# A convolution-and-attention trunk: two issues moved to another queue, four weight splits moved to another engine, one cost raised in the planner

## The chip, the cores and the metric

The kernel runs on one core of one Trainium2 chip. The metric is the device time of one execution in microseconds (us). Engines are named as in the profile: PE (TensorE), PEld (its weight loads), DVE (VectorE), ACT (ScalarE), POOL (GpSimd) and SP (SyncE, which only issues transfers). An engine's name with a q (ACTq, SPq) stands for its sequencer.

## The reference

One sequence of 512 tokens, width 1024, two layers, all in float32. Cut to its calls:

```python
for layer in range(2):
    if layer == 1:
        k_nope, k_rope, v = mla_shared_kv(h, ...)
    hn = rms_norm(h, mix_pre_g[layer])
    if layer < 1:
        m = conformer_conv(hn, ...)      # h @ w_pw1, gate, 31 taps per channel, layer norm, silu, @ w_pw2
    else:
        m = mla_attention(hn, ...)       # 8 heads, block-causal mask, softmax
    h = h + rms_norm(m, mix_post_g[layer])
    f = jnp.square(jax.nn.relu(rms_norm(h, ffn_pre_g[layer]) @ w_ff1[layer])) @ w_ff2[layer]
    h = h + rms_norm(f, ffn_post_g[layer])
```

In `conformer_conv` the product with `w_pw1` (1024 by 2048) gives a value half and a gate half; value times sigmoid(gate) goes through a causal convolution of 31 taps along the tokens, each channel by itself.

## The kernel before

**Split numbers.** Each float32 operand of a large matmul is held as a high part (`wh`, a rounded copy that ACT makes) and a lower part (`wl`, the rest). A product is three matmuls: high by high, lower by high, high by lower. Weights come in blocks of 128 by 1024 (512 KB) into five `raw` tiles; there are five `wh` tiles and six `wl` tiles. The function `weight` makes the lower part in one of two ways:

- DVE subtracts: `split` records an ACT copy of each 512 columns (raw to wh) and a DVE `tensor_tensor` (raw minus wh to wl).
- By transfer: ACT writes the rounded negative into `wl` and the rounded positive into `wh`, and then POOL issues a transfer that adds the block from DRAM onto `wl`.

The first pointwise weights are 16 blocks named `pw1`; block index 2c is the value half of channel group c (128 channels), and 2c+1 is its gate half. `lo_by_dma(name)` is true for all of `pw1`. Blocks 0 to 3 go the first way and blocks 4 to 15 the second.

**The convolution.** Eight channel groups c = 0 to 7. Groups 0, 1 and 3 take their 31 taps on DVE (`taps_vector`). Groups 2, 4, 5, 6 and 7 (`T_BLOCKS`) take them on PE (`taps_tensor`, 72 matmuls a group): the group's tokens must first be dealt so that four token phases lie side by side on the partitions. `deal_tokens` does this through DRAM: one 256 KB transfer writes the group's `u` to a `dealt` buffer, and when that has landed four 64 KB transfers read it back into `uu`. ACT issues both steps. An engine's instructions run in program order, so ACT stands still while one of these issues waits. The taps also need a matrix of weights: `load_toeplitz` loads nine 256 KB tiles for a group (`big<-cw` in the trace) on SP. `TAPS_AFTER` says where in PE's order the taps stand: group 2 after the products of c = 4, group 4 after c = 6, groups 5 and 6 after c = 7, and group 7 at the end, before the layer norm.

**Who orders the work.** The kernel does not issue instructions directly. A `Program` records them, `Program.cost` gives each an estimated duration in ns, and `schedule` simulates the five engines with those estimates and a simple model of transfers; of 16 rounds it keeps the order with the shortest simulated span, and `run` issues that order. Hence a changed estimate, or another engine for an operation, can change the order on every engine anywhere in the kernel. In the model a transfer is not placed more than `LEAD` = 16 us before it is due; on the chip SP issues as soon as its waits are met. All instructions carry the line of the one call that issues them (L640), so the trace is read by tiles and not by lines.

**Attention.** For each of 8 heads and 4 query blocks DVE adds the mask to the scores and reduces them to a row maximum in one `tensor_tensor_reduce`, and a DVE `tensor_scalar` on one column multiplies that maximum by a per-row weight.

Of the kernel before, what the change touches and what calls it, by code (L numbers as in the profile page):

```python
# [87 lines left out]
def lo_by_dma(name):  # L88
    if name[0] == "ff1":
        return name[2] == 0 and name[3] < 4  # L90
    if name[0] == "ff2":
        return name[1] == 0 and name[2] == 3 and name[3] in LAST_BY_DMA
    return name[0] in ("pw1", "pw2")
# [168 lines left out]
def _size(ap):  # L262
    n = 1
    for _, c in list(ap.ap)[1:]:
        n *= c
    return n
# [17 lines left out]
class Program:  # L284
# [68 lines left out]
    def cost(self, engine, method, kwargs, outs, ins):  # L353
        n = max([_size(a) for a in outs + ins] or [1])
        if method == "dma_start":
            return {"scalar": 380.0, "gpsimd": 900.0}.get(engine, 400.0)
        apart = {"vector": 0.77, "scalar": 0.6}.get(engine, 0.0) * n if any(
            list(a.ap)[-1][0] > 1 for a in outs + ins if _size(a) > 8
        ) else 0.0
        if engine in ("scalar", "vector") and ins and _size(ins[0]) > 8 and ins[0].ap[0][1] < P:  # L360
            apart += 120.0 if engine == "scalar" else 97.0
        if engine == "tensor":
            n = _size(outs[0])
            if ins[0].dtype == F32R:
                k = ins[0].ap[0][1]
                return max(120.0, n / 2.4 + 13.7) + (200.0 if k < P else 0.0)
            return 109.0 if method == "transpose" else max(222.0, n / 0.6 + 9)
        few = sum(_size(a) == 1 for a in ins) if n > 8 else 0
        psum = any(a.tensor.space == PSUM for a in outs + ins)
        if engine == "vector":  # L370
            wide = [a for a in ins if _size(a) > 1]
            rate = 1.042 if len(wide) > 1 or psum else 0.521
            return 68 + rate * n + 62 * few + apart
        if engine == "scalar" and n == 1:

            return 1350.0
        if engine == "scalar":
            few += "accum_out" in kwargs
            return (51 if psum else 94) + 0.833 * n + 93 * few + apart
        if engine == "gpsimd":  # L380
            return 150 + 2.1 * n
        return 450.0
# [68 lines left out]
    def schedule(self, tags):  # L451
# [49 lines left out]
        def better(op, e, cost, now):  # L501

            for f, _, _, _, c, held in op.ways:
                if f != e:
                    queue = sum(o.cost for _, _, o in avail[f] if not o.done and o is not op and o.rank < op.rank)
                    done = max(clock[f], now, port[0] if held else 0.0) + queue + c
                    if done < now + cost or (c > cost and done + SLACK < op.rank):
                        return True
            return False

        def urgent(op, e, cost, now):

            if op.held > HOLD or op.cost < 200:
                return False
            return any(
                at < now + 145 and not o.done and o.cost < TINY and o.rank < op.rank for at, _, o in future[e]
            )
# [126 lines left out]
def trunk(ctx: ExitStack, tc: tile.TileContext, xT, xN, wts, vec, along, rope, cw, out):  # L644
# [3 lines left out]
    nc = Program(tc.nc)  # L648
# [32 lines left out]
    n = VEC["mix_pre0"] + KT  # L681
# [35 lines left out]
    def scaled(name, src):  # L717

        lo, hi = ([big(F32R) for _ in range(2)] for _ in range(2))
        for o in range(2):  # L720
            raw = big()
            nc.sync.dma_start(out=raw, in_=src[:, o * T : (o + 1) * T])
            g0 = VEC[GAINS[name[0]]] + 4 * o
            gain = vt[:, g0 : g0 + 4].rearrange("p (k o) -> p k o", o=1).to_broadcast([P, 4, P])
            nc.vector.tensor_tensor(
                out=raw.rearrange("p (k m) -> p k m", m=P), in0=raw.rearrange("p (k m) -> p k m", m=P), in1=gain, op=ALU.mult
            )
            split(raw, slice(0, T), (hi[o], lo[o]))
        return hi, lo

    def weight(key):

        while key not in blocks:
            name, parts = USE[len(blocks)]
            i, n = BLK[parts[0][0]], _cols[BLK[parts[0][0]]]
            if name[0] in GAINS:
                blocks[name] = scaled(name, wts[i])
                continue
            raw, hi, lo = nc.tile(RAW), nc.tile(WH, F32R), nc.tile(WL, F32R)
            step = 256 if i < 2 else n  # L740
            for o in range(0, n, step):
                nc.sync.dma_start(out=raw[:, o : o + step], in_=wts[i, :, o : o + step])
            for other, sign in parts[1:]:
                if sign > 0:
                    nc.gpsimd.dma_start(out=raw, in_=wts[BLK[other]], accum_op=ALU.add)
                else:
                    second = nc.tile(RAW)
                    nc.sync.dma_start(out=second, in_=wts[BLK[other]])
                    for o in range(0, n, 512):
                        nc.vector.tensor_tensor(  # L750
                            out=raw[:, o : o + 512], in0=raw[:, o : o + 512], in1=second[:, o : o + 512], op=ALU.subtract
                        )
            src = raw if len(parts) > 1 else wts[i]
            if i >= 4 and lo_by_dma(name):

                for o in range(0, n, 512):
                    for dst, scale in ((lo, -1.0), (hi, 1.0)):
                        nc.scalar.activation(dst[:, o : o + 512], raw[:, o : o + 512], AF.Copy, scale=scale)
                nc.gpsimd.dma_start(out=lo, in_=src, accum_op=ALU.add)
            else:  # L760
                step = 256 if i < 2 else min(n, 512)
                engines = VG if name[0] in ATT else ("vector",)
                for o in range(0, n, step):
                    split(raw, slice(o, o + step), (hi, lo), engines=engines)
            blocks[name] = hi, lo
        return blocks[key]
# [5 lines left out]
    def products_of(keys, X, t0, n, nk=KT):  # L772

        w = [weight(key) for key in keys]
        pts = [nc.tile(MM) for _ in keys]
        for k in range(nk):
            for (hi, lo), pt in zip(w, pts):
                ks = slice(k * P, (k + 1) * P)
                if isinstance(hi, list):
                    hi, lo, ks = hi[k // 4], lo[k // 4], slice(k % 4 * P, (k % 4 + 1) * P)  # L780

                for j, (a, b) in enumerate(((hi, X[k][0]), (lo, X[k][0]), (hi, X[k][1]))):
                    nc.tensor.matmul(
                        pt[:, :n], lhsT=a[:, ks], rhs=b[:, t0 : t0 + n],
                        start=(k == 0 and j == 0), stop=(k == nk - 1 and j == 2),
                    )
        return pts

    def split(src, s, dst, d=None, engines=("vector",)):

        d = s if d is None else d
        nc.scalar.activation(dst[0][:, d], src[:, s], AF.Copy)
        nc.binary(engines, out=dst[1][:, d], in0=src[:, s], in1=dst[0][:, d].bitcast(F32), op=ALU.subtract)
# [167 lines left out]
    def feed_forward(layer, X, F):  # L961
# [6 lines left out]
        for q in range(4):  # L968
# [29 lines left out]
            def sides(q, p):  # L998
                return [weight(("ff2", layer, q, p, u)) for u in range(2)]
# [151 lines left out]
    def deal_tokens(c, up):  # L1151
        uu = UU[T_BLOCKS.index(c) % 3]
        dr = nc.tile(DEALT)
        nc.scalar.dma_start(out=dr.rearrange("p r m -> p (r m)"), in_=up)
        for r in range(R):
            nc.scalar.dma_start(
                out=uu[32 * r : 32 * r + 32, :, 8:], in_=dr[:, r, :].rearrange("(g c) m -> c g m", g=GROUPS)
            )

# [33 lines left out]
    for c in range(KT):  # L1193
# [5 lines left out]
        for j in T_BLOCKS:  # L1199
            if TAPS_AFTER.get(j) == c:  # L1200
                n = T_BLOCKS.index(j)
# [17 lines left out]
        if CONV[c] == "V":  # L1219
            taps_vector(c, u)  # L1220
        else:
            deal_tokens(c, u)
# [473 lines left out]
```

## Time and profile before

| | |
|---|---|
| median of three runs | 1064.88 us (1062.82 to 1067.0) |
| the profiled execution's own time | 1068.46 us |
| its span, first to last instruction | 1066.7 us |
| PE busy | 1045.5 us, 98% of the span |
| DVE, ACT, POOL busy | 764.1, 640.9, 141.6 us |
| mean granted PE clock | 0.993 of full speed |
| queue q1 (SP's), 16 engines' share | 40.9%, 150.15 MB |
| queue q0 (POOL's) | 25.6%, 49.29 MB |
| queue q10 (ACT's) | 1.1%, 3.68 MB |

The span is 1.8 us shorter than the profiled execution's own time, and that execution is 3.6 us above the median. A busy PE is not a PE at its peak: at a lower granted clock the same matmuls take longer and PE still counts as busy.

### The profile page before, as it was taken

The numbers are of one execution on the slowest core, as the hardware profiler recorded it, in microseconds if no ns is written. First come the engines' busy times: TensorE is split into PE (matmuls) and PEld (weight loads), VectorE is DVE, ScalarE is ACT, GpSimd is POOL, SyncE is SP. The second block draws the span as 40 slices with busy tenths as digits, with TensorE's granted clock in tenths as the row PEclk, the third lists the DMA queues.
The fourth block names the chain that finished last, engine by engine and source line by source line (L and its number), as shares of the span: only waits on it lengthen the run. The fifth ranks groups of instructions, "written<-read, shape, count | busy, mean of one in ns | idle before, by whom it ended". The sixth has DMA issues, their size and how long they took to land. (4 is left out here: it accounts for less than half of the span.)

```text
span 1066.7 us, 15181 instructions
## 1 busy us (share of the span) xinstructions
PE 1045.5 (98%) x5284; PEld 884.7 (83%) x5284; DVE 764.1 (72%) x1559; ACT 640.9 (60%) x1343; POOL 141.6 (13%) x165
## 2 busy tenths in 40 slices
PE   8989999999999999999999999999999999999996
PEld 7878988988888888888888888889888888888885
DVE  6497994857438737959988987547574495497698
ACT  8543497766545446545767877558565554454652
POOL 1110011100100100001104533301010010000010
PEclk9989999999999999999999999999999999999998
DMA  9995888657866848658923132557599388485684
GB/s 288 300 254 171 287 211 236 156 168 207 253 171 190 257 126 241 189 182 227 237 69 93 56 100 81 174 182 179 161 245 253 112 235 257 143 243 168 187 237 129
DMA packets 67613, 204.08 MB, mean 191 GB/s; under 512 B 7632, under 2 KB 13904, under 8 KB 67536
## 3 DMA queue, kind: packets, MB, share of 16 engines
q1 hardware_dynamic: 49680, 150.15, 40.9%
q0 software_dynamic: 13536, 49.29, 25.6%
q10 hardware_dynamic: 4320, 3.68, 1.1%
q8 instruction: 41, 0.67, 0.3%
q14 instruction: 36, 0.29, 0.1%
HBM read 197.58 MB, written 5.51 MB: 190 GB/s over the span
## 5 line engine op out<-in xcount | busy, mean ns | idle before, releaser
L640 PE MATMUL mm<-big,wh 128*128 128x512 f32 (+1 forms) x1512 | 441.1, 374 | 1.2 <-ACT wh L640 1.2
L640 PE MATMUL mm<-wh,big 128*128 128x512 f32 (+1 forms) x1216 | 374.7, 387 | 0.0
L640 ACT ACTIVATE wh<-raw 128x512 fp32r<-128x512 f32 (+2 forms) x444 | 251.0, 612 | 117.7 <-PE mm L640 73.8
L640 PEld LDWEIGHTS mm<-big,wh 128*128 128x128 f32 x1512 | 275.6, 188 | 52.4 <-ACT wh L640 1.5
L640 DVE TENSOR_TENSOR wl<-raw,wh 128x512 fp32r<-128x512 f32 (+1 forms) x356 | 227.7, 680 | 106.5 <-ACT wh L640 104.1
L640 PE MATMUL mm<-big,wl 128*128 128x512 f32 (+1 forms) x756 | 282.5, 374 | 0.0
L640 PEld LDWEIGHTS mm<-wh,big 128*128 128x128 f32 x1216 | 226.3, 188 | 46.9
L640 PE MATMUL mm<-wl,big 128*128 128x512 f32 (+1 forms) x608 | 234.9, 387 | 0.1
L640 PEld LDWEIGHTS mm<-big,wl 128*128 128x128 f32 x756 | 142.6, 189 | 25.7 <-DVE wl L640 0.5
L640 PEld LDWEIGHTS mm<-wl,big 128*128 128x128 f32 x608 | 114.2, 188 | 23.4 <-DVE wl L640 0.2
L640 POOL DMA_DIRECT2D raw<-wts x64 | 55.5, 867 | 572.7 <-DMA raw<-wts 190.4
L640 ACT ACTIVATE big<-tmp 128x256 f32<-128x256 f32 (+1 forms) x208 | 95.9, 493 | 43.2 <-DVE tmp L640 37.3
L640 DVE TENSOR_TENSOR big<-big,big 128x512 f32<-128x512 f32 (+4 forms) x103 | 69.8, 698 | 55.9 <-ACT big L640 55.6
L640 ACT ACTIVATE tmp<-mm 128x512 f32<-128x512 f32 (+1 forms) x75 | 41.7, 556 | 103.1 <-PE mm L640 102.0
L640 PE MATMUL mm<-big,big 128*128 128x256 f32 (+3 forms) x520 | 83.5, 310 | 1.8 <-DVE big L640 1.8
L640 PEld LDWEIGHTS mm<-big,big 128*128 128x128 f32 x520 | 73.1, 189 | 7.0 <-DVE big L640 2.3
L640 ACT ACTIVATE big<-mm 128x512 f32<-128x512 f32 (+5 forms) x106 | 56.6, 537 | 33.9 <-PE mm L640 32.9
L640 DVE TENSOR_TENSOR big<-tmp,big 128x512 fp32r<-128x512 f32 (+1 forms) x96 | 60.9, 642 | 15.3 <-ACT big L640 12.7
L640 DVE SCALAR_TENSOR_TENSOR big<-big,vt,big 128x512 fp32r<-128x512 f32 (+29 forms) x95 | 63.3, 736 | 8.0 <-ACT big L640 8.0
L640 DVE TENSOR_TENSOR big<-big,mm 128x512 f32<-128x512 f32 x96 | 63.7, 683 | 3.2 <-PE mm L640 2.8
L640 DVE TENSOR_TENSOR tmp<-big,big 128x512 f32<-128x512 f32 x80 | 53.3, 686 | 8.9 <-ACT big L640 8.9
L640 POOL DMA_DIRECT2D wl<-wts x30 | 26.1, 869 | 213.0 <-ACT wl L640 113.3
(90 smaller groups left out, 775.9 us busy)
## 6 DMA issues: line engine op xcount, KB each, us to landing
raw<-wts SPq DMA_DIRECT2D x222, 512.0 KB, 5.0
raw<-wts POOLq DMA_DIRECT2D x64, 512.0 KB, 7.9
wl<-wts POOLq DMA_DIRECT2D x30, 512.0 KB, 8.4
big<-cw SPq DMA_DIRECT2D x45, 256.0 KB, 5.6
big<-wts SPq DMA_DIRECT2D x12, 256.0 KB, 4.3
row<-along SPq DMA_DIRECT2D x5, 512.0 KB, 5.5
raw<-wts SPq DMA_DIRECT2D x12, 192.0 KB, 2.7
big<-xT SPq DMA_DIRECT2D x8, 256.0 KB, 4.2
```

The lines of the kernel that those rows point to most:

```text
L640: return f(*args, **kwargs)
```

## The change

Three edits.

1. In `deal_tokens` the four transfers of the second step (`uu<-dealt`) are issued by SP instead of ACT. The first step stays on ACT.
2. In `weight` the second way begins with block 8 instead of block 4: the lower parts of `pw1` blocks 4 to 7 (value and gate of groups 2 and 3) are made by DVE.
3. In `Program.cost` a DVE `tensor_tensor_reduce` counts 125 ns more, and a DVE `tensor_scalar` on fewer than 8 columns with more than one tensor input counts 62 ns more. No instruction changes by this; the planner's order may.

```diff
         if engine == "vector":
             wide = [a for a in ins if _size(a) > 1]
             rate = 1.042 if len(wide) > 1 or psum else 0.521
-            return 68 + rate * n + 62 * few + apart
+
+            more = 125 if method == "tensor_tensor_reduce" else 62 if method == "tensor_scalar" and n < 8 and len(ins) > 1 else 0
+            return 68 + rate * n + 62 * few + apart + more
...
             src = raw if len(parts) > 1 else wts[i]
-            if i >= 4 and lo_by_dma(name):
+            if i >= 8 and lo_by_dma(name):
...
         for r in range(R):
-            nc.scalar.dma_start(
+            nc.sync.dma_start(
                 out=uu[32 * r : 32 * r + 32, :, 8:], in_=dr[:, r, :].rearrange("(g c) m -> c g m", g=GROUPS)
             )
```

## The prediction

> **What bounds the kernel now.** I read the page's engine rows, then who waited for whom, then the busy time by stretch, then one stretch finely.
>
> ```profile
> span 1066.7 us, 15181 instructions
> PE 1045.5 (98%) x5284; PEld 884.7 (83%) x5284; DVE 764.1 (72%) x1559; ACT 640.9 (60%) x1343; POOL 141.6 (13%) x165
> PE mm L640 <- DMA uu<-dealt: 3.7, 1, 3.7
> 60.00:80.00 20.00, 16.31 (x96) 15.04 (x96) 20.00 (x32) 11.01 (x24) 2.59 (x3) 0.83 0.97 254
> 150.00:520.00 370.00, 369.92 (x1745) 308.15 (x1744) 253.07 (x485) 224.25 (x465) 37.98 (x46) 1.00 0.75 207
> 520.00:700.00 180.00, 176.50 (x1073) 155.68 (x1072) 141.33 (x387) 126.33 (x289) 57.19 (x51) 1.00 0.32 100
> ```
>
> The first two lines are the page; the third is PE's longest wait; the rest are stretches (start:end, length, busy us of PE, PEld, DVE, ACT, POOL, then granted clock, DMA share, GB/s). PE is busy 98% of the span, so time can be won only where PE is idle or runs at a lower clock. That is one place above all: from 60 to 80 us PE is idle 3.69 us and the clock is 0.83. The 370 us after 150 us (second pointwise product and first feed-forward) hold 0.08 us of PE idle.
>
> ```profile
> 67.30 11.04 PE L640 MATMUL mm<-uu,big 128*128 128x128 f32 x72 [3.69 <-DMA uu<-dealt]
> 107.78 8.20 PE L640 MATMUL mm<-uu,big 128*128 128x128 f32 x72
> 68.00:70.00 2.00, 2.00 (x12) 2.00 (x11) 2.00 (x5) 2.00 (x4) 0.79 (x2) 0.50 0.84 156
> 74.00:76.00 2.00, 2.00 (x20) 2.00 (x20) 2.00 (x4) 0.00 (x0) 0.00 (x0) 1.00 1.07 247
> ```
>
> These are PE's timeline and two short stretches. PE ends the products of group 4 at 63.6 us, waits 3.69 us for group 2's dealt tokens, and then does 72 tap matmuls in 11.04 us. The same 72 of group 4 take 8.20 us. The difference, 2.84 us, is the clock: 0.50 at 68 us and 1.00 at 74 us. The place costs 3.69 + 2.84 = 6.53 us.
>
> **Why the tokens are late.**
>
> ```profile
> 33.93 0.33 SPq L640 DMA_DIRECT2D big<-cw  x1
> big<-cw SPq DMA_DIRECT2D x1, 256.0 KB, 15.2
> 43.04 1.71 DVE L640 SCALAR_TENSOR_TENSOR big<-tmp,vt,tmp 128x512 f32<-128x512 f32 x2
> 49.18 0.33 ACTq L640 DMA_DIRECT2D dealt<-big  x1
> 49.61 0.64 ACT L640 ACTIVATE wl<-raw 128x512 fp32r<-128x512 f32 x1 [4.58 <-DVE big L640]
> dealt<-big ACTq DMA_DIRECT2D x1, 256.0 KB, 6.8
> 55.99 6.52 ACTq L640 DMA_DIRECT2D uu<-dealt  x4
> DMA to landing us min/median/max: 5.0/7.6/8.7
> q0 software_dynamic: 585, 2.14, 60.7%
> ```
>
> Timeline rows with, under the load of 33.93 and the dealt write, the issue view of the same transfer (KB, us to landing); then the landing view of group 2's four `uu` transfers; last, POOL's queue from 17 to 36 us. Group 2's `u` is the second of the two that DVE makes from 43.04 to 44.75 (the row of 49.61 names DVE, but that was long done). The write is issued at 49.18, just as an unrelated load issued at 33.93 lands (33.93 + 15.2 = 49.1), after ACT idled 4.58 us. It lands 6.8 us later; the first `uu` goes at 55.99, and the four issues stretch over 6.52 us instead of four times 0.4. I read these as waits for the landing of an older transfer: SP's and ACT's issues seem to share a few completion slots, so each is as late as the transfers are slow. And they are slow: POOL's additions alone hold 60.7% of the engines' time here.
>
> **The change part by part.**
>
> *Lower parts of blocks 4 to 7.*
>
> ```profile
> q0 software_dynamic: 13536, 49.29, 25.6%
> L640 POOL DMA_DIRECT2D raw<-wts x64 | 55.5, 867 | 572.7 <-DMA raw<-wts 190.4
> L640 POOL DMA_DIRECT2D wl<-wts x30 | 26.1, 869 | 213.0 <-ACT wl L640 113.3
> L640 DVE TENSOR_TENSOR wl<-raw,wh 128x512 fp32r<-128x512 f32 x4 | 2.8, 689 | 0.0
> L640 ACT ACTIVATE wl<-raw 128x512 fp32r<-128x512 f32 x22 | 12.6, 619 | 9.3 <-DMA raw<-wts 4.7 <-DVE big L640 4.6
> 20.00:40.00 20.00, 20.00 (x98) 16.72 (x97) 6.15 (x16) 13.71 (x25) 4.31 (x5) 1.00 1.05 257
> ```
>
> Removed: 4 POOL transfers of 0.87 us issue each and 8 ACT copies, 8 x 0.619 = 5.0 us. POOL's queue takes 25.6% of 1066.7 us for 64 + 30 transfers, so 2.9 us of all 16 engines each: 11.6 us of transfer time leave a stretch whose DMA share is 1.05. Added: 8 DVE subtractions, 8 x 0.689 = 5.5 us. They fall near 20 to 40 us, where DVE is busy 6.15 of 20 us; without that cover they would cost up to 5.5 us. I take 0 on the path; what counts is that loads issued before 49 us land earlier, by up to 11.6 us. Then the dealt write's 4.58 us wait goes, and the write itself is faster.
>
> *The second step on SP.* Twenty issues leave ACT and join SP:
>
> ```profile
> L640 ACTq DMA_DIRECT2D uu<-dealt x20: 309/409/677, 56.0 to 131.4; - x20
> 62.55 0.63 ACT L640 ACTIVATE wh<-raw 128x512 fp32r<-128x512 f32 x1 [8.56 <-DMA raw<-wts]
> 53.04 2.99 SPq L640 DMA_DIRECT2D big<-cw  x2
> big<-cw SPq DMA_DIRECT2D x1, 256.0 KB, 12.4
> dealt<-big ACTq DMA_DIRECT2D x1, 256.0 KB, 4.3
> ```
>
> 20 x 0.41 = 8.2 us of sequencer time move. ACT no longer stands 8.56 us before 62.55. SP now waits for each dealt write, 4.3 to 6.8 us as seen; queued behind it are `raw` block 15 and the `cw` tiles of the next tap group. In the trace SP had run ahead and put `cw` loads (issued from 53.04 on, 12.4 us to landing) in front of group 2's tokens, though these tiles are wanted only by the taps at 107.78. In program order on SP the four `uu` should stand ahead of most of them, because the model places a load no more than 16 us before it is due; the loads so held back have 107.78 - 53.04 = 54 us to spare, which hides the 4.3 to 6.8. Were that gone, the wait would move to the taps at 107.78, us for us. Group 2's tokens: the write leaves between 45.0 (ACT idle since then: 49.61 - 4.58) and 49.2, takes 4.3 to 6.8 us, four issues take 1.6 us, landing 5.0 to 7.6 us: 55.9 to 65.2 us against 63.6. I take the middle, 60.5: no wait, and without the wait no lower clock. Ends: a gain of 6.53 us, or a wait of 1.6 us still (gain 2.1, or 4.9 if so short a wait keeps the clock).
>
> *The planner's numbers.*
>
> ```profile
> L640 DVE CUSTOM_DVE_ANT_0 big<-mm,big 128x512 f32<-128x512 f32 x8 | 5.5, 685 | 0.3 <-PE mm L640 0.3
> L640 DVE DVE_READ_ACCUMULATOR2_ANT stat<- 128x1 f32 x32 | 2.7, 83 | 0.0
> L640 DVE TENSOR_SCALAR stat<-stat,wq 128x1 f32<-128x1 f32 x32 | 6.7, 211 | 0.6
> ```
>
> A masked maximum takes 685 + 83 = 768 ns; the formula gave 68 + 1.042 x 512 = 601 and now gives 726. The column product takes 211 and was put at 69, now 131. The estimates come nearer, so DVE's order in attention fits better, but the stretch 520 to 700 us holds only 3.5 us of PE idle. Bounds: -3.5 us and, for an order that happens to fit worse, +3.5. I take 0, since the work is the same.
>
> **Sum** against the profiled execution: 1068.46 - 3.69 - 2.84 + 0 + 0 = 1061.9 us. That execution is 3.6 us above the median; taken from the median, 1064.88 - 6.5 = 1058.4 us, which I forecast.
>
> A mean clock of 0.83 over the 20 us from 60 on is 20 x 0.17 = 3.4 us of clock lost, or 6.8 us at one half. The Trainium skill, "TensorE: Matmul & The Clock Gate" (The HAM clock gate), says the gate watches a free-running window of about 3.4 us and halves the clock after an idle one, and prices it at throttled time times one half. By that the clock costs 6.8 x 0.5 = 3.4 us instead of 2.84, and the sum is 1057.8. The trace's 0.50 agrees.
>
> **Rivals.**
>
> *Given back before the layer norm.*
>
> ```profile
> 120.00:140.00 20.00, 20.00 (x182) 20.00 (x181) 19.50 (x42) 15.72 (x34) 1.89 (x3) 1.00 0.78 241
> 98.97 0.75 DVE L640 SCALAR_TENSOR_TENSOR big<-tmp,vt,tmp 128x512 f32<-128x512 f32 x1 [3.32 <-ACT tmp L640]
> ```
>
> DVE is 97% busy there. If PE comes 6.5 us sooner and DVE does not, PE waits at the layer norm's sums. Against it: DVE's last long idle before, 3.32 us, waits for ACT, which here follows PE, so DVE comes sooner too. If half is lost the gain is 3.3 us: 1061.6.
>
> *The step does not help.* On SP's own queue the four `uu` follow whatever SP issued before them. In the trace, from ACT's queue, the first overtook a load: issued at 55.99, landed at most 8.7 us later, by 64.7, while a `cw` load issued at 53.04 landed 12.4 us later at 65.4. If SP has such loads in flight, the `uu` land after them, near 67, and the wait stays: 1064.9.
>
> The Trainium skill, "DMA: Bandwidth & Descriptors" (Queues, rings and completion order), says each DMA engine serves the queues that have work in turn, and one queue's descriptors in order. By that rule the move to SP loses ACT's turn and this rival holds wherever loads are in flight; the overtaking just shown agrees.
>
> *Slower: the next weights wait behind the last deal.*
>
> ```profile
> 120.15 1.34 SPq L640 DMA_DIRECT2D raw<-wts  x3
> 129.90 2.21 ACTq L640 DMA_DIRECT2D uu<-dealt  x4
> 145.20 0.86 POOL L640 DMA_DIRECT2D wl<-wts  x1 [4.50 <-ACT wl L640]
> wl<-wts POOLq DMA_DIRECT2D x1, 512.0 KB, 7.9
> 152.96 0.53 PE L640 MATMUL mm<-wh,big 128*128 128x512 f32 x1
> ```
>
> SP loads blocks of the second pointwise product from 120.15 on, before group 7's `uu` at 129.9. If the new order puts them after it, they go at 132 instead of 120, 12 us later, and the fourth block's lower part lands at 145.2 + 7.9 + 12 = 165 instead of 153. PE began that product at 152.96, would begin it at 146.4, and reaches its fourth block 3 x 12 matmuls x 0.21 us (369.92 / 1745) = 7.6 us on, at 154.0: a wait of 11 us and a lower clock again, 2.84, against 6.53 won: +7.3, 1072.2. It costs from a delay of 1 us on (153 against 154) and outweighs the gain from some 5 us on. For it: SP then stands still for the dealt write. Against: those loads become due before group 7's tokens exist.
>
> **How the numbers follow.** Main case 0.52, 1058.4 with its own range 1055.5 to 1061 (attention's order either way); given back in part 0.20, 1061.6; no help 0.15, 1064.9; slower 0.13, 1072.2. A measurement of this kernel tells about 0.5% (5.3 us) from no change, so faster means below 1059.6: 0.7 of the main case and a quarter of the second, 0.42. Slower: 0.13. Same: 0.45. The range 1055.5 to 1066 takes in all but the slower case and a little below.
>
> **What would show it.** Right: no PE wait on `uu<-dealt`, the first tap run in about 8.2 us at clock 1.00, PE reaching the taps of group 2 at 63 to 64 us, eight more DVE `wl` rows before 40 us, four fewer `wl<-wts` transfers, ACT without its 8.56 us wait. Wrong: a PE wait of over 1 us on `uu`, on `wl` near 147 us, or on DVE at the layer norm's sums; or PE idle between 520 and 700 us grown past 3.5 us.

## The result, and the profile after

The changed kernel takes 1072.34 us (median of five runs, 1070.59 to 1076.55) against 1064.88 for the kernel before: a ratio of 1.0077, 95% interval 1.0062 to 1.0093. Timed once more later it was 1073.49 against 1064.93, 1.009 [1.0074, 1.0105]. The forecast was 1058.4. The profile after is of the fastest of the five, the execution of 1070.59 us, and the profile before of one 3.6 us above its median, so the two profiles lie only 2.1 us apart. First the page of the profile after, then the same stretches as before (PE, PEld, DVE, ACT, POOL, clock, DMA share, GB/s).

```profile
span 1068.8 us, 15198 instructions
PE 1048.4 (98%) x5292; PEld 885.5 (83%) x5292; DVE 768.7 (72%) x1563; ACT 634.8 (59%) x1335; POOL 143.9 (13%) x165
q0 software_dynamic: 12960, 47.19, 24.6%
```

```profile
60.00:80.00 20.00, 20.00 (x126) 17.82 (x125) 20.00 (x33) 10.62 (x25) 2.59 (x3) 1.00 0.91 218
520.00:700.00 180.00, 173.78 (x1050) 153.98 (x1049) 134.67 (x367) 120.19 (x276) 61.32 (x55) 0.98 0.30 93
```

From 60 to 80 us everything came as forecast: PE is never idle and its clock is 1.00 (16.31 us and 0.83 before). From 520 to 700 us, in attention, PE's idle time grew from 3.50 to 6.22 us, and the clock fell to 0.98, which is about 180 x 0.02 = 3.6 us of clock.

The convolution in the timeline; the last line is the landing view of group 2's four reads:

```profile
45.58 0.34 ACTq L642 DMA_DIRECT2D dealt<-big  x1
47.64 1.95 SPq L642 DMA_DIRECT2D uu<-dealt  x4
64.22 8.20 PE L642 MATMUL mm<-uu,big 128*128 128x128 f32 x72
146.99 0.48 PE L642 MATMUL mm<-wh,big 128*128 128x512 f32 x1
DMA to landing us min/median/max: 3.9/4.3/4.4
```

Group 2's write leaves 3.6 us sooner than before (49.18), its four reads 8.35 us sooner (55.99), and they land in 4.3 us (median) instead of 7.6. PE takes the 72 taps at 64.22 without a wait, in 8.20 us. The second pointwise product begins at 146.99 instead of 152.96: 6 us ahead of the profile before.

Where it went, in the timeline of the changed kernel near 587 us (VectorE, GpSimd, PE):

```profile
585.83 1.34 DVE L642 TENSOR_TENSOR stat<-stat 128x4 f32<-128x4 f32 x2
587.21 0.59 DVE L642 SCALAR_TENSOR_TENSOR stat<-stat 128x4 f32<-128x4 f32 x1
587.83 3.05 DVE L642 TENSOR_TENSOR big<-big,big 64x256 fp32r<-64x256 f32 x2
585.65 1.31 POOL L642 TENSOR_TENSOR big<-big,big 64x512 fp32r<-64x512 f32 x1
587.04 4.43 POOL L642 TENSOR_TENSOR wl<-raw,wh 128x256 fp32r<-128x256 f32 x4
587.25 0.52 PE L642 MATMUL mm<-big,big 128*128 128x256 f32 x3
590.94 4.96 PE L642 MATMUL mm<-big,big 128*128 128x128 f32 x14 [3.17 <-DVE big L642]
```

The same work in the kernel before:

```profile
588.48 1.28 POOL L640 TENSOR_TENSOR big<-big,big 64x512 fp32r<-64x512 f32 x1 [1.08 <-ACT big L640]
592.25 1.96 PE L640 MATMUL mm<-big,big 128*128 128x256 f32 x11 [0.74 <-DVE big L640]
595.34 0.69 DVE L640 TENSOR_TENSOR big<-big,big 64x512 fp32r<-64x512 f32 x1
```

The first scores need the lower rotary query part of head 0, one 64x512 subtraction. The planner may give it to VectorE or GpSimd. Before, GpSimd made it at 588.48, and head 1's, not needed yet, followed on VectorE at 595.34. In the new order GpSimd makes head 1's first (585.65), and head 0's stands on VectorE behind a chain of small `stat` operations and a 64x256 subtraction, as the second of the two in the row of 587.83. It ends at 590.88; PE starts at 590.94 after 3.17 us of idle, and the 14 matmuls then take 4.96 us at half clock.

### The profile page after: what moved, and what is told of

Read it like the earlier page. It is cut to its first block, busy times and chain, and to the rows that moved or that the text cites. A ratio compares the mean times of both kernels' runs of the same rounds, so it can differ in the third digit from the quotient of the medians.

```text
span 1068.8 us, 15198 instructions
## 1 busy us (share of the span) xinstructions
PE 1048.4 (98%) x5292; PEld 885.5 (83%) x5292; DVE 768.7 (72%) x1563; ACT 634.8 (59%) x1335; POOL 143.9 (13%) x165
## 4 chain that ended last, share of the span: by engine, by line
PE 76%; DVE 3%; ACT 3%; issue 1%; DVEq 0%
PE mm L642 75%; PE bc L642 2%; DVE big L642 2%; ACT big L642 1%; DVE stat L642 1%; ACT junk L642 1%; ACT wh L642 0%; DVE h L642 0%; ACT wl L642 0%; DVE wl L642 0%; DVEq L1694 0%; ACT tmp L642 0%; DVEq L642 0%
## 5 line engine op out<-in xcount | busy, mean ns | idle before, releaser
L642 PEld LDWEIGHTS mm<-big,wh 128*128 128x128 f32 x1512 | 276.4, 189 | 53.5 <-ACT wh L642 1.5
L642 DVE TENSOR_TENSOR wl<-raw,wh 128x512 fp32r<-128x512 f32 (+1 forms) x360 | 230.8, 682 | 115.6 <-ACT wh L642 111.7
L642 POOL DMA_DIRECT2D wl<-wts x26 | 23.0, 883 | 198.3 <-ACT wl L642 156.7
```

The lines of the kernel that those rows point to most:

```text
L642: return f(*args, **kwargs)
```

## The experiments

All times are medians of six or twelve executions, with the ratio to the kernel before on the same chip and its interval; experiments 8, 10 and 12 are single executions. "Old order" means: the planner plans the kernel before, and an edit is made only when an instruction is issued, so every engine keeps its order.

**1. Both edits of instructions, in the old order (frozen_both).** The diff is cut: the lines in `weight` that set `instead` are left out.

```diff
         for op, (engine, method, args, kwargs, *_) in sequence:
+            if method == "dma_start" and engine == "scalar" and any(t.tag.name[:2] == "uu" for t in op.tiles):
+                engine = "sync"
+            instead = getattr(op, "instead", 0)   # set in weight() for pw1 blocks 4 to 7
+            if instead is None:
+                continue
             self.issue(...)
+            if instead:
+                self.nc.vector.tensor_tensor(**{k: real(a) for k, a in instead.items()})
```

> The planner makes the order of the kernel before, with that kernel's estimates; only when the instructions are issued are the four uu transfers given to SP instead of ACT, and for blocks 4 to 7 each high-part copy is followed by a DVE subtraction while the negative copy and the adding transfer are left out. So edits 1 and 2 are made and every other instruction keeps its place. Theory A (re-planning: the convolution wins some 6 us and all of the loss comes from the new order of attention): 1064.9 - 6.5 = 1058.4, between 1056 and 1061; PE idle from 520 to 700 us as before, 3.5 us. Theory B (the moved issues and the subtractions cost later by themselves, through SP's queue or the transfers' timing): no gain, 1064 to 1073, with the loss again between 572 and 613 us.

Measured 1065.03 us, 1.0006 [0.9992, 1.0021]. The time is theory B's, no gain, but the loss in attention is theory A's: from 520 to 700 us PE is idle 3.45 us, as in the kernel before (3.50), against 6.22 in the changed kernel. The wait of group 2 is gone too, yet nothing is won: PE now waits ahead of group 7's taps.

```profile
520.00:700.00 180.00, 176.55 (x1069) 155.71 (x1068) 141.16 (x380) 127.43 (x288) 57.84 (x52) 1.00 0.32 97
60.00:80.00 20.00, 20.00 (x126) 17.82 (x125) 20.00 (x32) 10.74 (x25) 2.49 (x3) 1.00 0.83 236
133.01 1.24 PE L647 MATMUL mm<-uu,big 128*128 128x128 f32 x9 [1.26 <-DMA uu<-dealt]
```

**2. The same two edits, planned anew with the old estimates (plan_12).** The changed kernel without the lines of `Program.cost`.

> Edits 1 and 2 as in the change, planned anew, but the planner's costs of the kernel before (no edit 3). If the raised costs made the bad order of attention: 1057 to 1062. If edits 1 and 2 already shift the plan enough to spoil it: 1067 to 1074, with a PE wait of over 2 us somewhere between 520 and 700 us. Theory B: 1067 to 1074 too, with the wait at the same place as in the changed kernel.

Measured 1068.29 us, 1.0034 [1.002, 1.0048]. The time is in the range given for a plan that edits 1 and 2 alone already shift, but the wait of over 2 us that went with it is not there: PE's longest wait between 520 and 700 us is 1.1 us, and it is idle 5.12 us in all. The two edits are the same as in experiment 1; 3.3 us come from the order alone.

**3. Only the estimates (cost_only).** The kernel before with the changed lines of `Program.cost`.

> Edit 3 alone, planned anew; the convolution's stall of 3.7 us stays. If the raised costs made the bad order of attention: 1064.9 + 7 = 1072, 1069 to 1075. If they are harmless: 1062 to 1067, with PE idle from 520 to 700 us at 2 to 5 us.

Measured 1066.43 us, 1.0016 [1.0002, 1.0029]. This is inside the range for harmless estimates, with PE idle 4.26 us from 520 to 700 us, but the interval lies above 1. No instruction differs, so this too is the price of an order. The profile of this kernel says something of the first step as well: with the convolution's code unchanged, PE's wait at group 2 is half as long.

```profile
PE mm L641 <- DMA big<-cw: 1.8, 1, 1.8
60.00:80.00 20.00, 18.23 (x117) 16.08 (x116) 20.00 (x32) 14.56 (x33) 3.45 (x4) 1.00 1.01 276
```

It waits 1.8 us, and the clock stays at 1.00. The row names a `cw` load, but the last of the four reads was issued at 60.5 and took 5.3 us, and the taps begin at 65.87: PE waited for the tokens here too.

**4. Only the second step on SP, in the old order (frozen_sync).** The first two added lines of experiment 1.

> The order of the kernel before, with only the four uu transfers given to SP at issue (edit 1 without edit 2). If being on SP ahead of the cw loads is enough: the tokens land by 63.6 us and the time is 1057 to 1061. If the relief of the transfers by edit 2 is what brings the tokens in time: the dealt write still leaves near 49 us and lands near 56, a wait of 1 to 4 us stays, 1062 to 1067.

Measured 1062.61 us, 0.9979 [0.9964, 0.9994]: 2.3 us faster, the best of the study. Neither expectation fits whole: the time is in the second's range, but the wait at group 2 is gone. The write leaves at 46.3 us, not near 49; SP issues the four reads from 52.3 to 54.5 us, and they land in 4.9 us (median), so the tokens are there by 58.5 us without the second edit. The profile is of its slowest execution (1067.96) and shows 3.74 us of idle ahead of group 7's taps.

**5. The changed kernel with one place of attention mended (after_mend).** After planning, two entries change engines and two move. In words, not code:

```diff
-  gpsimd: head 1's 64x512 query part      # early
-  vector: 64x256 key part, head 0's 64x512 query part, four 128x256 evacuations
+  gpsimd: head 0's 64x512 query part      # early
+  vector: four 128x256 evacuations, 64x256 key part, head 1's 64x512 query part
```

> The changed kernel with three VectorE operations moved, nothing else: head 0's lower query part (64x512) goes to GpSimd in the place where GpSimd made head 1's, head 1's goes to VectorE, and that one and the 64x256 lower key part of the odd heads stand behind the four 128x256 evacuations of the first values instead of ahead of them. Theory A (one bad place in the new order of attention): the 3.17 us wait of PE at 587.5 and the 6.83 us at clock 0.50 behind it (3.4 us) go together; PE idle near 588 below 1 us, clock 1.00 from 520 to 700 us, time 1072.3 - 6.5 = about 1066, within 1064.5 to 1068. Rival B (the loss is spread over the whole new order, or the wait moves on to head 1's scores some 8 us later): 1069.5 to 1072.5, with a wait of over 2 us still between 588 and 602.

Measured 1069.83 us, 1.0039 [1.0025, 1.0053]. Theory A's place is right and its size too large: PE's longest wait for VectorE is now 1.2 us, the two near the old place are 0.43 us (at 587.94) and 0.83 us (at 599.12), and the clock in attention is 1.00. The changed kernel's row for this stretch stands ahead of the mended one's (PE busy, clock, DMA share, GB/s).

```profile
520.00:720.00 200.00, 193.56 (x1137) 0.98 0.35 107
```

```profile
PE bc L683 <- DVE big L683: 2.9, 5, 1.2
520.00:720.00 200.00, 195.84 (x1163) 1.00 0.36 111
```

The interval lies below both of the changed kernel (1.0062 to 1.0093 and 1.0074 to 1.0105), and the middle moves by 0.0038 to 0.0051: 4 to 5.4 us for this one place, where 6.5 was expected. Rival B is right in the rest: 4.2 us above the kernel before remain by the ratio (4.7 by the medians), spread over other places.

**6. Only the lower parts by VectorE, in the old order (frozen_lower).** The other added lines of experiment 1.

> The kernel before in its own order on every engine, with only the lower parts of blocks 4 to 7 made by VectorE. Theory A (less transfer work lets the dealt tokens of group 2 land sooner, and the eight subtractions are hidden): wait for uu near 63 us below 0.5 us, 2 to 3 us faster than before, 1062 to 1063. Rival B (VectorE's 5.5 us of subtractions come back as a wait, or group 2's tokens were never held by those transfers): 1065 or more, with a wait of VectorE's or of uu of over 1 us by 64 us.

Measured 1063.83 us, 0.9983 [0.997, 0.9997]. Theory A holds in direction, with 1.3 us where 2 to 3 were expected. There is no wait at group 2 at all (no idle time stands in the row of its taps), and attention is as in the kernel before:

```profile
26.60 1.16 PE L645 MATMUL bc<-ident,stat 128*128 128x128 f32 x8 [0.51 <-DVE stat L645]
65.79 8.20 PE L645 MATMUL mm<-uu,big 128*128 128x128 f32 x72
520.00:720.00 200.00, 196.55 (x1165) 1.00 0.36 110
```

Experiment 4 has no wait there either, so each edit alone takes it away. But here the subtractions are not wholly hidden. PE waits 0.51 us for VectorE at 26.60 us, a wait that only the runs of the old order with this edit show (1, 6 and 11). In these PE reaches group 2's taps at 65.4 to 65.8 us; with the reads on SP alone (4, 7 and 12) it does at 63.8 to 64.6. A second edit thus finds no wait left to remove, and this one costs about 1 us, so doing both wins nothing more.

**7. The second step on SP for groups 2, 4, 5 and 6, on ACT for group 7 (frozen_sync_4).** Experiment 4 with a count: only the first 16 reads move.

> The kernel before in its own order, with the second step of the dealing issued by SP for groups 2, 4, 5 and 6, and by ACT for group 7 as before. Theory A (SP's own order delays only group 7's tokens, where its profile showed 3.74 us of PE idle at 130 us): no wait above 0.7 us near 130, 1061 to 1062.5 and no execution above 1066. Rival B (that wait has nothing to do with the issuing engine, as the last group's tokens are just late): 1062.6 like the kernel with all five groups on SP, with slow executions of 1065 to 1068 among the twelve.

Measured 1063.78 us, 0.9987 [0.9973, 1.0001]. Theory A is wrong. With ACT issuing group 7's reads, PE still waits for group 7's tokens:

```profile
132.17 1.05 PE L644 MATMUL mm<-uu,big 128*128 128x128 f32 x7 [2.27 <-DMA uu<-dealt]
uu<-dealt SPq DMA_DIRECT2D x16, 64.0 KB, 4.0
uu<-dealt ACTq DMA_DIRECT2D x4, 64.0 KB, 6.9
```

So it is not group 7's own place on SP that makes its tokens late. SP still issues the reads of groups 4 to 6 here; experiment 11 shows what that does.

**8. The kernel before again (before_again).** No edit.

> The kernel before once more, for its profile. Theory A (the wait of 3.69 us for uu and the stretch at clock 0.50 belong to the executions near 1068; the usual one, near 1065, waits 1 to 2.5 us and keeps its clock): an execution near 1065 shows a wait for uu of 1 to 2.5 us at 64 us and clock 0.95 or more from 60 to 80 us. Rival B (the wait is 3.7 us in every execution and the times differ elsewhere): 3.3 us or more and clock 0.83 at any time.

It took 1068.3 us, again one of the long executions, so neither theory was tested on an ordinary one. The wait was 2.47 us and the clock 0.91:

```profile
67.25 9.90 PE L640 MATMUL mm<-uu,big 128*128 128x128 f32 x72 [2.47 <-DMA uu<-dealt]
60.00:80.00 20.00, 17.53 (x107) 15.83 (x106) 20.00 (x32) 12.16 (x27) 2.59 (x3) 0.91 0.97 256
120.00:150.00 30.00, 28.44 (x238) 27.82 (x237) 28.20 (x74) 25.85 (x56) 3.93 (x5) 0.95 0.80 210
```

The last row is the stretch of the layer norm, where the clock fell too; in the first profile it was 1.00 there. What an ordinary execution does was not seen. The clocks give a hint. Of 64 executions of the kernel before, timed beside experiments 1 to 8, four had a mean clock of 0.994 and took 1068.1 to 1068.8 us; the 32 with 0.997 or 0.998 took 1062.2 to 1066.3. A difference of 0.003 in clock is 3.2 us of 1065. The other 28, at 0.995 and 0.996, took 1063.3 to 1069.2, so the clock is not the whole of it.

**9. The changed kernel again (after_again).** No edit.

> The changed kernel once more, timed beside the kernel before and profiled. Theory A (the first profile of it, an execution of 1070.6 us, was a good one; the usual one also loses at the layer norm, as two other newly planned kernels did): an execution of 1072 us or more shows 2 to 3 us of PE idle between 138 and 144 us and a clock below 0.97 from 120 to 150, and again 3.2 us of idle near 587; median 1072 to 1073. Rival B (the wait near 587 is itself the accident of one execution): less than 1 us of idle there, and the median's excess over the kernel before stands elsewhere.

Measured 1073.49 us, 1.009 [1.0074, 1.0105]; the profiled execution's span is 1070.6. Theory A holds on both counts, with the median half a us above its range. The wait in attention is there again, the same to 0.01 us, and PE now waits at the layer norm's sums too:

```profile
120.00:150.00 30.00, 27.69 (x227) 27.13 (x226) 27.17 (x82) 24.53 (x55) 4.33 (x5) 0.94 0.99 288
140.03 0.84 PE L642 MATMUL bc<-col,big 128*128 128x128 f32 x4 [0.96 <-DVE big L642]
142.21 0.80 PE L642 MATMUL bc<-col,tmp 128*128 128x128 f32 x4 [1.35 <-ACT tmp L642]
149.10 0.47 PE L642 MATMUL mm<-wh,big 128*128 128x512 f32 x1
593.07 4.32 PE L642 MATMUL mm<-big,big 128*128 128x128 f32 x14 [3.18 <-DVE big L642]
```

The same two waits in the old order, with only the lower parts moved (experiment 6):

```profile
141.22 0.84 PE L645 MATMUL bc<-col,big 128*128 128x128 f32 x4 [0.39 <-DVE big L645]
142.55 0.71 PE L645 MATMUL bc<-col,tmp 128*128 128x128 f32 x4 [0.49 <-ACT tmp L645]
148.16 0.50 PE L645 MATMUL mm<-wh,big 128*128 128x512 f32 x1
```

PE's waits at the sums are 2.31 us against 0.88, and 30 x 0.06 = 1.8 us of clock go. PE finished the taps 1.8 us sooner than in experiment 6 and begins the next product 0.9 us later. The loss of clock there is not the new order's own: the kernel before had 0.95 in this stretch in experiment 8, after waits of 0.88 and 0.66 us, and experiment 11, in the old order, 0.94. The first profile of the changed kernel had only 0.83 and 0.36 us here; the two other kernels planned anew with these edits (experiments 2 and 5) had 1.22 and 1.34.

**10. The changed kernel with its large tiles in reverse places (after_places).**

```diff
+        for tag in tags:
+            if tag.name == "big":
+                for p in reversed(range(tag.count)):
+                    tag.make(f"big__{p}", F32, p)
```

> The changed kernel with the 48 large tiles laid out in SBUF in the reverse order, nothing else. It asks why the first feed-forward takes 319.7 us in both kernels that were planned anew with the first two edits and 318.4 in the other four, with the same matmuls. Theory A (the place of the tiles sets the length of a matmul): the stretch from the first matmul of the feed-forward to the transposes behind it changes by over 0.3 us, either way. Rival B (the order of the engines sets it): 319.6 to 319.8 us.

The feed-forward ran from 200.15 to 519.90 us: 319.75. Rival B: the places do not matter. What makes the matmuls of this stretch slower in the new order stays open; the counts in 260 us show it, first the kernel before, then this one.

```profile
245.00:505.00 260.00, 260.00 (x1139) 213.55 (x1138) 175.99 (x286) 141.94 (x279) 22.85 (x27) 1.00 0.74 206
```

```profile
245.00:505.00 260.00, 260.00 (x1135) 212.77 (x1134) 174.56 (x284) 142.54 (x279) 22.19 (x26) 1.00 0.73 205
```

Four matmuls fewer at 0.228 us are 0.9 us; over the whole feed-forward it is 1.2 us. The one execution took 1075.93 us, and no conclusion is drawn from that.

**11. Both edits in the old order, but only group 2's reads on SP (frozen_both_1).** Experiment 1 with the first four reads moved.

> The kernel before in its own order, with the lower parts of blocks 4 to 7 by VectorE and the second step of the dealing on SP for group 2 alone; the other four groups stay on ACT. Theory A (what is won at group 2 is mostly waited off at group 7, whose tokens land near 132 us whoever issues them): 1062.5 to 1064, no better than either edit alone, with PE at group 7's taps between 130.5 and 132.5. Rival B (SP's queue is what holds group 7 back, and only together with the earlier PE): 1061 to 1062.3, group 7's taps before 130.5 without a wait.

Measured 1064.59 us, 0.9992 [0.9982, 1.0002]. As theory A says it is no better than either edit alone, but its reason fails here: PE reached group 7's taps at 131.31 without a wait. In experiment 1, which differs only in the reads of groups 4 to 7, it waited 1.26 us. The views of group 7's reads (KB, us to landing), of the stretch around them (PE busy, clock, DMA share, GB/s) and of SP's issue of the next product's blocks, first of experiment 1, then of this one:

```profile
uu<-dealt SPq DMA_DIRECT2D x4, 64.0 KB, 6.0
126.00:132.00 6.00, 5.75 (x52) 1.00 1.06 344
120.34 5.52 SPq L647 DMA_DIRECT2D raw<-wts  x3
```

```profile
uu<-dealt ACTq DMA_DIRECT2D x4, 64.0 KB, 2.0
126.00:132.00 6.00, 6.00 (x57) 1.00 0.32 61
115.07 1.29 SPq L649 DMA_DIRECT2D raw<-wts  x3
```

With the reads on SP, SP issues the `raw` blocks of the next product some 5 us later, and they are in flight beside group 7's reads, which take 6.0 us instead of 2.0. In experiment 7 the share was 1.03 and ACT's reads took 6.9. So the later loads go with the late tokens in these profiles; no run moved the loads alone.

**12. Experiment 4 again, for its profile (frozen_sync_again).**

> The kernel before in its own order with the second step of the dealing on SP for all five groups, once more, for the profile of an ordinary execution (the first profile was of its slowest, 1068.0 us). Theory A (an ordinary execution reaches group 7's taps at 131 to 132 us after a wait of 1 to 2.5 us and keeps its clock; the 3.74 us and the halved clock were that execution's own): 1061.3 to 1063.5 us, clock 0.97 or more from 120 to 150 us. Rival B (the wait of 3.7 us and the halved clock are there each time): 1065.5 us or more and clock 0.89.

It took 1067.47 us, with 2.75 us of idle ahead of group 7's taps (3.74 in the first profile) and a clock of 0.94 from 120 to 150 us. Both profiles of this kernel are of long executions, so it stays open what an ordinary one, at 1062.6, does there.

## Why the prediction was wrong

*The wait at group 2: right in its mechanism, mis-sized in its price.* Issue, landing, the taps at 64.22 and their 8.20 us came as written, and the last read landed by 53.5 us instead of the 60.5 taken. VectorE has 20 `wl` rows before 40 us instead of 12, and GpSimd's additions fell from 30 to 26. But the step that wrote "1064.88 - 6.5" took a price from an execution of 1068.46 us and subtracted it from the median of others. Both profiled executions of the kernel before are long ones, with waits of 3.69 and 2.47 us; in experiment 3, in another order and at 1067.11 us, the same code of the convolution waited 1.77 us with a full clock. That an ordinary execution pays less there fits this, and is not shown. What is shown is the net gain in the old order: 1.3 to 2.3 us with one edit (experiments 4 and 6) and none with both (experiment 1), where 6.5 was taken. The subtractions, put at 0 on the path, cost about 1 us of that in the old order (experiment 6); in the new one PE reaches the taps at 64.22.

*Given back.* The rival of 0.20 put the loss before the layer norm. In experiment 9 PE waits there 2.31 us where the old order had 0.88, but it also comes sooner, and by the next product it is only 0.9 us behind experiment 6. The text argued that VectorE would come sooner because ACT follows PE; in the new order ACT's and VectorE's parts of the sums come later than PE does. In the old order group 7's tokens took a part instead (experiments 1, 4, 7 and 12).

*The planner's numbers: the step that failed.* "I take 0, since the work is the same", with bounds of 3.5 us either way from PE's idle time of 3.5 us in attention. That idle time bounds what a better order can win. It says nothing on what a worse one can lose, and the text used it for both. From experiment 1 to the changed kernel, with the same work in another order, it is 7.3 us (1065.03 to 1072.34); the gain that did not come makes up the other 6.6 us between forecast and result (1058.4 to 1065.03). Nor is it one edit's matter: every edit makes the planner order all engines anew. Alone, the estimates cost 1.5 us (experiment 3), and the first two edits lose 3.3 us by being planned (2 against 1). All three together give the order with the bad place, worth 4 to 5.4 us (experiment 5). The list of signs did name PE idle above 3.5 us between 520 and 700 us; it was 6.22.

*The other rivals.* "The step does not help" is wrong: group 2's reads went 8.35 us sooner and landed in 4.3 us. "Slower: the next weights wait" did not happen either, since PE began the second pointwise product with no wait for weights; that SP's loads slide behind the dealing was seen in the old order (experiment 11), where they met group 7's tokens. The kernel became slower by a mechanism that no rival named.

*What remains.* From the old order with both edits (1.0006) to the changed kernel (1.0077, 1.009) there are 7.6 to 8.9 us. Experiment 1 (profiled at 1065.41 us) and experiment 9 (1072.34 us) show where: PE's first matmul of the first feed-forward, the transposes near its end, and PE's last matmul.

```profile
195.23 0.28 PE L647 MATMUL mm<-big,wh 128*128 128x256 f32 x1
513.65 0.41 PE L647 MATMUL bc<-ident,h 128*128 128x128 f32 x2
1052.90 0.39 PE L647 MATMUL mm<-wh,big 128*128 128x512 f32 x1
```

```profile
195.94 0.28 PE L642 MATMUL mm<-big,wh 128*128 128x256 f32 x1
515.70 0.38 PE L642 MATMUL bc<-ident,h 128*128 128x128 f32 x2
1060.58 0.39 PE L642 MATMUL mm<-wh,big 128*128 128x512 f32 x1
```

PE is 0.7 us later at the feed-forward, loses 1.3 us in it and 5.6 us behind it. So the layer norm adds little, because PE comes to it sooner in the new order. Of the 5.6 us the mended place takes 4 to 5.4. The feed-forward's part and the small waits elsewhere in attention were seen in profiles and not tested by an edit that removes them.

## What to carry to other kernels

Where a planner orders the instructions, price an edit twice: once for its own work, and once as a new order of everything behind it. The idle time of a stage bounds a gain there, not a loss. Hold the old order fixed and make the edit at issue; that tells the two apart in one run. And before a stall of one profile is subtracted from a median, look at the execution's own time and clock: 3.6 us above the median was the warning, and it was written down and not used.

## What was not expected of the hardware

VectorE's operations on two SBUF inputs stretch beside GpSimd's. In the changed kernel the 64x256 and 64x512 subtractions took 3.05 us together, and two operations on four columns 1.34, while GpSimd ran one `tensor_tensor` after another. Where none of GpSimd's was under way as they began, the same shapes are short: 64x256 took 0.63 us at 583.47 and, in the kernel before, 64x512 took 0.69 and four columns 0.15 (at 593.09). The Trainium skill, "SBUF — State Buffer" (SBUF: two separate sides), says that a VectorE operation with two SBUF inputs and a GpSimd operation that reads SBUF hold a shared port pair exclusively, for the whole instruction. The rows agree, down to operations of four columns. This is no effect of the change: in the kernel before, two operations on four columns took 1.44 us at 588.55 beside GpSimd's 64x512. At the short lengths the three VectorE rows near 587 us would take 1.8 us instead of 4.98, an estimate, and the 3.2 us between are about the length of PE's wait; no run tested this apart from the order. The planner has a rule for such pairs (`port` in `schedule`), and the order with the bad place is its own.

The clock halved after short waits and stayed after a longer one. In experiment 9 it fell at the layer norm after waits of 0.96 and 1.35 us among small matmuls, and in experiment 8 after 0.88 and 0.66, while in experiment 7 a single wait of 2.27 us left it at 1.00. None of these is idle for the 3.4 us by which the prediction priced the clock. What decides it is not shown.
